# GpSimd's request queue held in program order in an expert layer that streams both of its tables

## The chip, the cores and the metric

The kernel runs on one core of one Trainium2 chip. The metric is the device time of one launch in microseconds. Five engines work side by side, each with its own instruction queue: TensorE (PE, with its weight loads shown as PEld), VectorE (DVE), ScalarE (ACT), GpSimd (POOL) and SyncE (SP). SP issues the plain loads from device memory, POOL issues the indirect ones, which fetch one table row per partition. The two share the core's 16 DMA engines.

## The reference

The program is one step of a two-layer encoder over 384 tokens: 256 of a prompt and 128 of eight sample streams. Layer 0 has a state-space mixer, layer 1 windowed attention; each is followed by a PEER channel mixer, and that is all that matters here:

```
s1, s2 = q1 @ sub_k1.T, q2 @ sub_k2.T          # 8 heads, 128 keys each
top 16 of s1, top 16 of s2, top 16 of the sums  # 128 experts of 16384 for each token
act = gelu(sum_d u_tab[eid] * x)                # one dot product per token and expert
out = sum_k (gate * act)[k] * v_tab[eid[k]]     # weighted sum of value rows
```

Both tables have 16384 rows of 1024 floats, 64 MB each, for each layer.

## The kernel before

**Two ways through the tables.** For the 256 prompt tokens the kernel computes all 16384 dot products densely, as matmuls of 128 blocks of the u table (`u_products`, lines 168 to 170), masks them with the gates (`w_prep`, `w_apply`, `w_mult`) and multiplies the result with 128 blocks of the v table (`v_products`, line 183). For the 128 sample tokens it fetches the chosen rows: each is one indirect DMA of 128 rows of 4 KB, 512 KB in all, issued by POOL at line 1250 (`gather`).

**Three kinds of request on POOL's queue.** `fetch_u` fetches a u row set, which DVE multiplies with the tokens in `u_item` (line 1299); 128 of them a layer, in a ring of 3 buffers (`gath`), and of 4 in the second part (`gathx`). `fetch_v` fetches a value row set into a freed place of the big arrays G0 and G1; four of them make a quad, which PE multiplies with small selection matrices `cm` in `v_quad` (line 1370); 24 quads, so 96 sets a layer. `fetch_item` fetches a value row set which DVE adds up itself in `v_item` (lines 1323 and 1325); 32 a layer. `items_end` (line 1339) adds DVE's sum to the quads' sum on PE. POOL also issues four plain DMAs a group of tokens (`load_group`, line 1071), one for the reload of the residual `h` (line 1618), and computes a few reciprocal roots.

**The steps.** Time within a layer is counted in steps s of one table block. Steps 0 to 63 are the first half of u, 64 to 127 the second half, 128 to 255 the values. In each step of the second half the program goes: gates of the step before, load and split of the blocks to come (`split`, lines 132 on ACT and 133 on DVE), products, `quads(s)`, `quads_ahead(s)` (which prepares `cm`), `w_prep`, `tick(s)`, and in the values `item_tick(s)`. A split is done two steps ahead of its products.

**What sets the requests.** `U_DUE` says how many u items are done by which step; `tick` fetches a set 2 or 3 items ahead of the item and runs it whatever the budget. `quads` issues one value set a step, if the budget `room` isn't negative and a place in `V_SLOTS` is free long enough (`v_slot`); a place is free again two steps after its quad. `V_DUE` holds the step of each quad: `quads_ahead` prepares it in the step before, `v_quad` runs in it. `PACE` refills the budget in each step, and each request takes 1 from it.

**What sets the order.** A planner arranges each engine's instructions by its own estimate of when they can start, unless they are held. From step 64 to the end of a layer the context `in_order` holds PE, DVE and ACT in program order (`HELD`, line 38). POOL and SP are not held: the planner may put a POOL request ahead of others that the program has before it, as long as its place is free. `load_group(1)` stands just ahead of step 64, outside the held stretch.

Of the kernel before, what the change touches and what calls it, by code (L numbers as in the profile page):

```python
# [26 lines left out]
HELD = (mybir.EngineType.PE, mybir.EngineType.DVE, mybir.EngineType.Activation)  # L27
# [16 lines left out]
TG = P // GR  # L44
# [12 lines left out]
GD = 2  # L57
QR = [r for r in range(32) if r // RG != GD]
I_DUE = (206, 250)
PACE = 1.6  # L60
AHEAD = 2 * 64 - 5
U_DUE = ((64, 22), (128, 68), (192, 115), (206, P))
V_DUE = [82, 85, 90, 95, 102, 148, 156, 162, 167, 171, 177, 181, 186, 192, 197, 203,
         213, 218, 223, 228, 233, 237, 243, 247]
V_SLOTS = [(1, e, 66, 64 + e) for e in range(28, 60, 4)] + [(0, e, 128 + e + 5, 256) for e in (0, 4, 8, 12, 20, 24, 28, 32, 56, 60)] + [(0, 16, 209, 256)]


# [1 line left out]
def encoder_step(ctx: ExitStack, tc: tile.TileContext, t_in, t_out):  # L69
# [14 lines left out]
    pin = tc.keep_in_program_order  # L84

    @contextmanager
    def in_order():

        traced = nc.cur_bb.bb.instructions
        n, last = len(traced), {}  # L90
        for i in traced:
            last[i.engine] = i
        kind = mybir.DependencyInfo(mybir.DependencyClass.NoSync, mybir.DependencyReason.DATA)
        yield
        for i in traced[n:]:
            if i.engine in HELD:
                if i.engine in last:
                    tc.add_manual_dep(i, last[i.engine].name, kind, reason="in order")
                last[i.engine] = i
# [844 lines left out]
    def peer(l):  # L944
        with ExitStack() as c:
# [56 lines left out]
            with in_order():  # L1002
                wq = [split_raw(raws[0])]
                sums(0, 0)
                sums(0, 1)
                sums(1, 0)
                nrm.rstd(0)
                nrm.scale(0, xn[0])
                sums(1, 1)
                sums(2, 0)  # L1010
                nrm.rstd(1)
                sums(2, 1)
                nrm.scale(1, xn[1])
                nrm.rstd(2)
                nrm.scale(2, xn[2], 2)
                for b in range(2):
                    turn(range(6), [b])
# [252 lines left out]
            def v_slot(n, s):  # L1270
                return next((k for *k, s0, s1 in V_SLOTS if s0 <= s and V_DUE[n // 4] <= s1 and taken.get(tuple(k), 0) <= s), None)

# [37 lines left out]
            def fetch_item(e2):  # L1310
                while spare[0] < 56 and spare[0] + 4 <= e2:
                    slots.append(spare[0])
                    spare[0] += 4
                if slots and done["g"] < TG and done["g"] < done["i"] + 3 and room[0] >= 0:
                    room[0] -= 1
                    j, e = done["g"], slots.pop(0)
                    items[j] = e, gather(G[0][:, e:e + 4].rearrange("p e t -> p (e t)"), t_in["p_v"], eidU[:, GD, j:j + 1])
                    done["g"] += 1

            def v_item(j):  # L1320
                e, row = items.pop(j)
                if j == 0:
                    pin(dve.tensor_scalar(acc, row, cU[:, 0:1], None, op0=OP.mult))
                else:
                    pin(dve.scalar_tensor_tensor(acc, row, cU[:, j:j + 1], acc, op0=OP.mult, op1=OP.add))
                slots.append(e)

            def items_sel():
                sel = T(one, [P, 4, 32], F32, tag="cm", bufs=2)
                dve.memset(sel, 0.0)  # L1330
                dve.tensor_reduce(sel[:, :, GD * RG:GD * RG + RG], ident.rearrange("p (q c r) -> p c r q", c=4, r=RG),
                                  axis=AX.X, op=OP.add)
                sels.append(sel)

            def items_end():
                sel = sels.pop()
                for hf in range(2):
                    for q in (3, 2, 1, 0):
                        pin(pe.matmul(out_s[hf][32 * q:32 * q + 32, :], sel[:, q], acc[:, hf * 512:hf * 512 + 512],
                                      start=False, stop=True, tile_position=(0, 32 * q)))  # L1340

            def item_tick(s):
                want = min(TG, max(0, TG * (s + 1 - I_DUE[0]) // (I_DUE[1] - I_DUE[0])))
                while done["i"] < want:
                    v_item(done["i"])
                    done["i"] += 1
                    if done["i"] == TG - 2:
                        items_sel()
                    if done["i"] == TG:
                        items_end()  # L1350
                if s >= I_DUE[0] - 4:
                    fetch_item(s - 2 * HE)

            def quad_prep(r):
                g = r // RG
                cm = T(one, [P, 4, 32], F32, tag="cm", bufs=2)
                dve.scalar_tensor_tensor(cm, ioh[:, None, 0:32].to_broadcast([P, 4, 32]), float(r),
                                         coef[g][:, r % RG::RG].unsqueeze(2).to_broadcast([P, 4, 32]),
                                         op0=OP.is_equal, op1=OP.mult)
                return r, cm  # L1360
# [12 lines left out]
            def u_weights(e2):  # L1373

                if e2 in NATIVE:
                    return load_raw(t_in["u_t"][l, e2]), None
                return load_split(t_in["u_t"][l, e2])
# [93 lines left out]
            done = {"u": 0, "v": 0, "f": 0, "i": 0, "g": 0, "c": 0}  # L1471
            cms, sels = [], []
# [4 lines left out]
            def tick(s):  # L1477

                room[0] = min(room[0] + PACE, PACE)
                s0, n0 = start[0], 0  # L1480
# [20 lines left out]
            def quads(s):  # L1501

                while cms:
                    v_quad(*cms.pop(0), s)
                    done["v"] += 1
                first = 4 * sum(d < 2 * HE for d in V_DUE)
                if (done["f"] < (first if s < 2 * HE else 4 * len(QR)) and room[0] >= 0 and v_slot(done["f"], s)):
# [3 lines left out]
            def quads_ahead(s):  # L1511

                while done["c"] < len(QR) and V_DUE[done["c"]] <= s + 1:
                    cms.append(quad_prep(QR[done["c"]]))
# [44 lines left out]

            turn_of.pop("v", None)  # L1560
            wt = u_weights(HE)
            held = in_order()
            held.__enter__()
            for e2 in range(HE):
                if mult:
# [27 lines left out]
            for e2 in range(2 * HE):  # L1593
# [17 lines left out]
                if e2 in w_at:  # L1611
                    made.append(w_prep(1, w_at[e2]))
                tick(2 * HE + e2)
                item_tick(2 * HE + e2)
                if e2 == AHEAD - 1:
                    lent.__exit__(None, None, None)
# [35 lines left out]

    mamba(t_in["x"].rearrange("(b p) d -> p b d", p=P))
    peer(0)
    attention()
    peer(1)
    final()

# [95 lines left out]
```

## Time and profile before

| | |
|---|---|
| median of 3 runs | 2385.33 us (2384.52 to 2387.32) |
| the profiled execution | 2389.37 us, span 2387.5 us |
| PE busy | 2317.2 us, 97% |
| DVE, ACT, POOL busy | 82%, 52%, 32% |
| mean DMA rate | 272 GB/s |
| second half of u and values, layer 0 | about 664 to 1306 us |
| the same, layer 1 | about 1732 to 2377 us |

A busy PE covers nearly the whole span, so what can be won without taking work from PE is the time in which it stands still or runs at a lower clock. The granted clock (PEclk) is a share of the full 2.4 GHz; 0.5 is the lower level of 1.2 GHz, and values between are means over a stretch that has both. The DMA share is the mean busy share of the 16 DMA engines, and it can show slightly over 1.

### The profile page before, as it was taken

The page shows a single profiled execution, that of the slowest core. Times are in us where ns is not written, and L with a number is a line of the kernel's source. Part 1 is how long each engine was busy: PE and PEld are TensorE (multiplying, and loading weights), DVE is VectorE, ACT ScalarE, POOL GpSimd, SP SyncE. Part 2 cuts the span into 40 slices and gives each one's busy share as a digit, 9 for nine tenths or more (in the row PEclk, how much of TensorE's full clock was granted, in tenths as well). Part 3 has the DMA queues.
Part 4 walks back from the last instruction along what each step waited for, and adds up shares of the span by engine and source line. Part 5 has one row for each costly group of instructions (what it writes and reads, how often), then busy time and mean ns, then how long its engine had stood idle before and what let it go on. Part 6 is the DMA issues. An engine that isn't in the chain of part 4 may idle for free.

```text
span 2387.5 us, 44460 instructions
## 1 busy us (share of the span) xinstructions
PE 2317.2 (97%) x16607; PEld 1984.0 (83%) x16607; DVE 1964.6 (82%) x4227; ACT 1252.3 (52%) x2428; POOL 772.6 (32%) x779
## 2 busy tenths in 40 slices
PE   7999999999989999999999999999989999999998
PEld 7899988999988997667777778999988997667676
DVE  5888855979978999888777676979978999887776
ACT  5656534344466766554444555344466766554343
POOL 2122200011144334556462200012144334566461
PEclk9999999999999999999999999999999999999999
DMA  5454435367689889999996515366789889999996
GB/s 200 174 193 172 150 142 170 117 205 254 237 311 343 302 300 336 382 399 405 377 414 253 166 65 180 124 218 241 249 316 343 295 306 333 395 395 413 343 417 250
DMA packets 177943, 649.75 MB, mean 272 GB/s; under 512 B 21232, under 2 KB 23136, under 8 KB 175328
## 3 DMA queue, kind: packets, MB, share of 16 engines
q1 hardware_dynamic: 100800, 365.85, 42.1%
q0 software_dynamic: 76928, 281.07, 31.4%
q8 instruction: 130, 2.13, 0.4%
q14 instruction: 85, 0.70, 0.1%
HBM read 630.62 MB, written 18.06 MB: 272 GB/s over the span
## 4 chain that ended last, share of the span: by engine, by line
PE 82%; DVE 6%; DMA 4%; issue 3%; ACT 2%; POOL 2%; another core or an unknown queue 0%; SPq 0%; POOLq 0%; DVEq 0%; ACTq 0%
PE bank L183 27%; PE bank L168 12%; PE bank L170 12%; PE bank L169 11%; PE bank L1370 3%; PE bank L1458 3%; PE bank L1383 2%; PE bank L1425 2%; DVE lo L133 2%; DMA gath<-in_p_u,eidU 1%; POOL G L1250 1%; DMA gathx<-in_p_u,eidU 1%; ACT hi L132 1%; DMA ab<-acum_rows 1%; PE bank L522 1%
## 5 line engine op out<-in xcount | busy, mean ns | idle before, releaser
L132 ACT CAST hi<-raw 128x1024 fp32r<-128x1024 f32 (+1 forms) x475 | 496.0, 1045 | 687.6 <-PE bank L169 322.7
L133 DVE TENSOR_TENSOR lo<-raw,hi 128x1024 fp32r<-128x1024 f32 (+1 forms) x475 | 576.0, 1213 | 171.8 <-ACT hi L132 159.0
L1250 POOL DMA_INDIRECT gath<-in_p_u,eidU x226 | 292.8, 1296 | 787.6 <-DVE gath L1299 455.3
L170 PE MATMUL bank<-xhi,lo 128*128 128x256 f32 (+1 forms) x1344 | 396.5, 295 | 17.0 <-DVE lo L133 15.8
L168 PE MATMUL bank<-xhi,hi 128*128 128x256 f32 (+1 forms) x1344 | 403.7, 301 | 0.4 <-issue 0.4
L169 PE MATMUL bank<-xlo,hi 128*128 128x256 f32 (+1 forms) x1344 | 394.8, 294 | 0.1
L1250 POOL DMA_INDIRECT G<-in_p_v,eidT x192 | 232.6, 1212 | 138.6 <-PE bank L1370 80.6
L170 PEld LDWEIGHTS bank<-xhi,lo 128*128 128x128 f32 x1344 | 255.7, 190 | 21.2 <-DVE lo L133 18.9
L168 PEld LDWEIGHTS bank<-xhi,hi 128*128 128x128 f32 x1344 | 256.0, 190 | 13.4 <-issue 7.9
L169 PEld LDWEIGHTS bank<-xlo,hi 128*128 128x128 f32 x1344 | 255.8, 190 | 1.5 <-issue 0.8
L168 PE MATMUL bank<-qhi,hi 128*128 128x256 f32 (+1 forms) x784 | 232.3, 296 | 0.0
L170 PE MATMUL bank<-qhi,lo 128*128 128x256 f32 (+1 forms) x784 | 227.0, 290 | 2.4 <-DVE lo L133 2.4
L169 PE MATMUL bank<-qlo,hi 128*128 128x256 f32 (+1 forms) x784 | 228.1, 291 | 0.0
L1413 ACT ACTIVATE oa<-ioh,e2T 128x128 f16<-128x128 f16 x512 | 163.6, 392 | 90.7 <-PE bank L1425 77.4
L132 ACT CAST hix<-raw 128x1024 fp32r<-128x1024 f32 x118 | 124.0, 1051 | 165.4 <-PE bank L183 76.9
L183 PE MATMUL bank<-hi,phi 128*128 128x512 f32 x632 | 204.6, 403 | 1.5 <-ACT phi L132 1.5
L183 PE MATMUL bank<-lo,phi 128*128 128x512 f32 x632 | 197.6, 392 | 0.9 <-DVE lo L133 0.9
L183 PE MATMUL bank<-hi,plo 128*128 128x512 f32 x632 | 196.3, 390 | 0.0
L133 DVE TENSOR_TENSOR lox<-raw,hix 128x1024 fp32r<-128x1024 f32 x118 | 144.1, 1221 | 16.8 <-ACT hix L132 16.5
L1299 DVE SCALAR_TENSOR_TENSOR gath<-gath,xg 128x1024 f32<-128x1024 f32 x114 | 138.7, 1217 | 16.5 <-DMA gath<-in_p_u,eidU 16.5
L183 PEld LDWEIGHTS bank<-hi,phi 128*128 128x128 f32 x632 | 113.9, 188 | 45.6 <-ACT phi L132 14.1
L170 PEld LDWEIGHTS bank<-qhi,lo 128*128 128x128 f32 x784 | 147.8, 188 | 2.8 <-DVE lo L133 2.8
(395 smaller groups left out, 5186.5 us busy)
## 6 DMA issues: line engine op xcount, KB each, us to landing
raw<-in_u_t SPq DMA_DIRECT2D x256, 512.0 KB
raw<-in_p_v SPq DMA_DIRECT2D x256, 512.0 KB
raw<-in_w_in SPq DMA_DIRECT2D x32, 512.0 KB
raw<-in_p_w_q SPq DMA_DIRECT2D x32, 512.0 KB
raw<-in_w_z SPq DMA_DIRECT2D x16, 512.0 KB
s<-in_state_ssm SPq DMA_DIRECT2D x8, 1024.0 KB
out_sm_ssm<-s SPq DMA_DIRECT2D x8, 1024.0 KB
raw<-in_w_out SPq DMA_DIRECT2D x16, 512.0 KB
```

The source lines that it names most:

```text
L132: act.copy(hi, raw)
L133: dve.tensor_tensor(lo, raw, hi32, op=OP.subtract)
L168: pe.matmul(ps, whi[:, s], xhi[:, k, c0:c1], start=(k == 0), stop=False)
L169: pe.matmul(ps, whi[:, s], xlo[:, k, c0:c1], start=False, stop=False)
L170: pe.matmul(ps, wlo[:, s], xhi[:, k, c0:c1], start=False, stop=(k == KD - 1))
L183: mm = pe.matmul(halves[hf], x, w[:, hf * n:(hf + 1) * n], start=s_, stop=e_)
L1250: pool.indirect_dma_start(out=tile_, out_offset=None, in_=tab, in_offset=bass.IndirectOffsetOnAxis(ap=idx, axis=0))
L1299: pin(dve.scalar_tensor_tensor(tile_, tile_, 1.0, xg[g], op0=OP.mult, op1=OP.mult, accum_out=au[g][:, j:j + 1]))
L1370: pe.matmul(out_s[hf][32 * q:32 * q + 32, :], cm[:, q], rows[q][:, hf * 512:hf * 512 + 512], start=(r == 0), stop=False, tile_position=(0, ...
L1383: pe.matmul(ps, wt[0][:, k * P:(k + 1) * P], xf[:, k], start=(k == 0), stop=(k == KD - 1))
L1413: act.activation(a[:, i], ioh, AF.Square, scale=-1.0, bias=e2T[:, t, 0:1])
L1458: pe.matmul(accs[b][hf], G[e2 // HE][:, e2 % HE, b * P:(b + 1) * P], wt[0][:, hf * 512:hf * 512 + 512], start=False, stop=False)
```

## The change

Three things are changed, and no instruction is added or taken away.

1. `in_order` takes the engines to hold as an argument, and the stretch from step 64 to the end of each layer now holds POOL as well. The dependencies that it adds are for the planner alone; they are no waits on the chip.
2. `PACE` goes from 1.6 to 1.5, and the steps of the value quads (`V_DUE`) are laid out anew: the first three stay, most of the others come 0 to 8 steps later, and the last is at 252 where it was at 247.
3. `items_end` now comes only when the last quad is done as well, which moves it from step 249 to step 252.

```
-PACE = 1.6
+PACE = 1.5
-V_DUE = [82, 85, 90, 95, 102, 148, 156, 162, 167, 171, 177, 181, 186, 192, 197, 203,
-         213, 218, 223, 228, 233, 237, 243, 247]
+V_DUE = [82, 85, 90, 96, 103, 148, 156, 162, 167, 173, 178, 183, 188, 193, 199, 211,
+         217, 222, 227, 232, 237, 243, 247, 252]
...
-    def in_order():
+    def in_order(engines=HELD):
...
         for i in traced[n:]:
-            if i.engine in HELD:
+            if i.engine in engines:
                 if i.engine in last:
                     tc.add_manual_dep(i, last[i.engine].name, kind, reason="in order")
                 last[i.engine] = i
...
-                    if done["i"] == TG:
-                        items_end()
+                if sels and done["i"] == TG and done["v"] == len(QR):
+                    items_end()
...
-            held = in_order()
+            held = in_order(HELD + (mybir.EngineType.Pool,))
```

## Rows read from the trace of the kernel before

**Rows 1.** The page's first part: busy time, share of the span and instructions of each engine.

```profile
PE 2317.2 (97%) x16607; PEld 1984.0 (83%) x16607; DVE 1964.6 (82%) x4227; ACT 1252.3 (52%) x2428; POOL 772.6 (32%) x779
```

**Rows 2.** Busy time by stretch, second half of u and values: stretch, its length, busy us of each engine (instructions), granted clock, DMA share, GB/s. Layer 0 first, then layer 1 from 1734.

```profile
666.00:702.00 36.00, 29.00 (x261) 27.80 (x260) 25.29 (x39) 19.52 (x41) 18.59 (x17) 0.91 0.91 343
756.00:762.00 6.00, 4.93 (x46) 4.52 (x44) 4.75 (x8) 4.52 (x10) 0.57 (x1) 1.00 1.03 414
895.00:1136.00 241.00, 241.00 (x1451) 167.82 (x1450) 213.50 (x360) 136.15 (x273) 132.68 (x109) 1.00 0.98 381
1136.00:1145.00 9.00, 6.56 (x37) 4.00 (x36) 4.72 (x8) 2.71 (x4) 3.75 (x4) 1.00 1.03 418
1145.00:1300.00 155.00, 155.00 (x749) 115.69 (x748) 119.41 (x150) 65.27 (x97) 74.43 (x57) 1.00 0.95 367
...
1734.00:1771.00 37.00, 29.60 (x268) 28.53 (x266) 25.96 (x39) 19.62 (x42) 18.68 (x17) 0.91 0.90 337
1826.00:1832.00 6.00, 5.17 (x55) 4.93 (x54) 5.92 (x11) 4.82 (x12) 0.29 (x1) 1.00 1.02 419
2205.00:2220.00 15.00, 10.88 (x49) 6.48 (x48) 9.40 (x16) 3.91 (x6) 5.15 (x4) 0.89 0.89 338
```

**Rows 3.** Who waited for whom: engine and line, what it waited for, us in total, times, longest. PE in the two layers' first part, then PE in their last part, then DVE at the start of layer 0's stretch.

```profile
PE bank L170 <- DVE lo L133: 7.7, 5, 5.7
...
PE bank L170 <- DVE lo L133: 7.2, 3, 5.9
...
PE bank L1370 <- DVE cm L1357: 2.4, 1, 2.4
...
PE bank L1370 <- DVE cm L1357: 4.1, 1, 4.1
...
DVE gath L1299 <- DMA gath<-in_p_u,eidU: 5.6, 1, 5.6
```

**Rows 4.** POOL's instructions in order of time at the start of layer 0's stretch: start, us, line, what, idle time before. Six more value requests stand between the second row and the third.

```profile
666.66 2.03 POOL L1071 DMA_DIRECT2D G<-xrow  x4 [2.02 <-ACT xlo L1534]
669.00 1.99 POOL L1250 DMA_INDIRECT G<-in_p_v,eidT  x1 [0.30 <-issue]
...
680.00 0.94 POOL L1250 DMA_INDIRECT G<-in_p_v,eidT  x1 [0.30 <-issue]
681.24 1.85 POOL L1250 DMA_INDIRECT gath<-in_p_u,eidU  x1 [0.30 <-issue]
```

**Rows 5.** Pieces of the chain that ended last, in order of time: start, us, what. For a DMA the time runs from its issue to its landing.

```profile
669.00 6.63 DMA G<-in_p_v,eidT
681.24 10.85 DMA gath<-in_p_u,eidU
...
951.07 1.85 PE bank L1370 x16
...
1105.53 1.95 PE bank L1370 x16
...
1129.21 9.92 DMA gathx<-in_p_u,eidU
...
1188.16 1.85 PE bank L1370 x16
...
1749.46 11.16 DMA gath<-in_p_u,eidU
...
2196.98 12.26 DMA gathx<-in_p_u,eidU
2212.23 3.45 PE bank L1370 x16
```

**Rows 6.** Busy time by stretch as in Rows 2, in pieces of 6 us after the halts at the two starts.

```profile
696.00:702.00 6.00, 6.00 (x36) 6.00 (x36) 4.22 (x7) 1.33 (x2) 0.84 (x1) 0.64 0.86 335
702.00:708.00 6.00, 6.00 (x66) 5.96 (x65) 5.57 (x10) 4.47 (x9) 1.03 (x2) 1.00 0.77 227
...
1764.00:1770.00 6.00, 6.00 (x35) 6.00 (x34) 4.22 (x8) 1.33 (x2) 0.94 (x1) 0.60 0.94 343
```

**Rows 7.** Instructions in order of time at the start of layer 0's stretch: DVE's u item of step 65, and ACT's cast of a u block at 680, with the idle time before it.

```profile
671.57 1.22 DVE L1299 SCALAR_TENSOR_TENSOR gath<-gath,xg 128x1024 f32<-128x1024 f32 x1
...
679.98 1.05 ACT L132 CAST hi<-raw 128x1024 fp32r<-128x1024 f32 x1 [3.30 <-remote]
```

**Rows 8.** POOL's instructions in order of time before the late halt in layer 1.

```profile
2191.78 0.94 POOL L1250 DMA_INDIRECT G<-in_p_v,eidT  x1 [1.56 <-PE bank L1370]
...
2195.52 1.16 POOL L1250 DMA_INDIRECT G<-in_p_v,eidT  x1 [0.30 <-DMA gath<-in_p_u,eidU]
2196.98 1.98 POOL L1250 DMA_INDIRECT gathx<-in_p_u,eidU  x1 [0.30 <-issue]
```

**Rows 9.** Groups of POOL's requests over the whole span: line, what, count, busy us and mean ns of one, idle time before and its causes.

```profile
L1250 POOL DMA_INDIRECT gath<-in_p_u,eidU x226 | 292.8, 1296 | 787.6 <-DVE gath L1299 455.3
L1250 POOL DMA_INDIRECT G<-in_p_v,eidT x192 | 232.6, 1212 | 138.6 <-PE bank L1370 80.6
```

**Rows 10.** The end of layer 1: two pieces of the chain, then DVE's first sums of the residual (line 1468) from the order of time.

```profile
2359.07 1.85 PE bank L1339 x16
2360.92 11.16 PE bank L183 x48
...
2374.66 1.28 DVE L1468 TENSOR_TENSOR h<-h,bank 128x512 f32<-128x512 f32 x2
```

## The prediction

> **What bounds the kernel now.** I read the busy shares first: PE is busy for 2317 of 2387.5 us [rows 1], and the change takes no work from it. So the question is where PE stands still inside the two stretches that the change touches, and the view by stretch says it: in layer 0, 36.0 - 29.0 = 7.0 us in the first 36 us, 1.07 us at 756, 2.44 us at 1136, and nothing in the two long pieces beside it; in layer 1, 37.0 - 29.6 = 7.4, 0.83 and 4.12 us [rows 2]. That is 22.9 us. The clock adds to it: after each starting halt PE runs for a few us at a lower granted clock, 0.64 and 0.60 in the mean of 6 us, and gets 36 and 35 products done where the next 6 us have 66 [rows 6]. That is 30/66 and 31/66 of 6 us, 2.7 and 2.8 us. In the late halt of layer 1 one quad took 3.45 us where others take 1.95 [rows 5], 1.5 us more. All that can be won without less work on PE is 22.9 + 5.5 + 1.5 = 29.9 us.
>
> Next, who holds PE there. At both starts it waits 5.7 and 5.9 us for line 133, DVE's low half of a u block [rows 3], though the block itself isn't late: DVE works in order, and just before it waits 5.6 us for a u row set [rows 3]. That set was issued at 681.24, because POOL had first issued `load_group` at 666.66 and then eight value requests from 669.00 to 680.00 [rows 4]. By the code those eight belong to steps 66 to 74, and their quads to steps 82 and 85: the planner took them first since their places were free. The u set then took 10.85 us to land, in layer 1 11.16 [rows 5]. The two late halts have the same form. A u set went out at 1129.21 and at 2196.98 and landed 9.92 and 12.26 us later [rows 5]; in layer 1 four value requests stand before it, from 2191.78 on [rows 8], which by the code belong to steps 202 to 210 (for the quad of step 213); DVE waits, its `cm` is late, and PE waits 2.4 and 4.1 us for that [rows 3].
>
> **The change, part by part.**
>
> *POOL in program order.* I followed `tick`, `quads`, `v_slot` and `fetch_item` by hand through steps 64 to 255 with the new constants. Behind `load_group(1)` comes the u set of step 65, then one value set, the u set of step 66, and so on in turn; the eighth value request comes in step 75. One request occupies POOL for 1.2 to 1.3 us [rows 9] and 0.3 us of issue [rows 4]. The u set that was issued at 681.24 now has three requests in front of it (`load_group`, one u set, one value set) and a buffer that comes free when DVE has done the item of step 65, begun at 671.57 [rows 7]. So it goes out in about 673, some 8 us earlier, and the halt for it, 5.6 us on DVE, is covered. I take the whole of 5.7 + 5.9 on PE and the clock with it, 5.5: 17.1 us. What is late next are the u blocks: ACT waited 3.30 us for one at 680 [rows 7], and that accounts for the other 1.3 + 1.5 us of the two starts. In that time the DMA engines had nine requests and the blocks; now it is seven and the blocks. I take half of the 2.8, 1.4 us. Bounds: nothing (the blocks wait as before), or all.
>
> The Trainium skill, "DMA: Bandwidth & Descriptors", section "Queues, rings and completion order", says that each DMA engine takes turns between the queues that have work, a packet at a time. By that rule SP's blocks had their share of turns however many value requests POOL had queued, so fewer of these would not bring them sooner: the 1.4 us would be zero, and the sum 1.4 us smaller. The rule leaves the u set's own delay as it is, since that stood behind the eight in the same queue.
>
> *The halts at 756 and 1826* (1.07 and 0.83 us) come in a stretch at DMA share 1.03 [rows 2] after two batches of four value requests. In program order these are one a step. Half of it, 1.0 us; bounds 0 and 1.9.
>
> *The late halts.* The u sets of steps 192 to 206 come at 13 in 14 steps. The value requests beside them become fewer: the quad of step 203 goes to 211 and the next from 213 to 217, so steps 200 to 207 have 9 requests of all kinds where the code had 10, and none from later steps are put in front. Four requests fewer are 4 x 0.524 MB / 420 GB/s = 5 us of DMA time (the most that rows 2 show is 419), against waits of 2.4 and 4.1. The total is 2.4 + 4.1 + 1.5 = 8.0 us; I take two thirds, 5.4, because the ring of four buffers still has to turn 0.93 sets a step. Bounds 0 and 8.0.
>
> *The new waits.* Held in order, a request whose buffer isn't free keeps all behind it back. Queued behind it are the other kinds of gather; who waits for those are DVE (u and item rows) and PE (quads). A u set waits for the item 3 or 4 before it, so POOL can be ahead of the program by one to two steps at most. Counted so, the 96 value sets have at least 4.9 steps from the latest release that stands before them to the end of their quad's step; 12 of them have 4.9 or 5.0, the others more. A step is (1105.53 - 951.07) / 44 = 3.5 us from step 148 to 192, and (1188.16 - 1105.53) / 26 = 3.2 with its halt, 3.1 without, from 192 to 218 [rows 5]. So the least is 4.9 x 3.1 = 15.2 us, less two requests that POOL issues before it, 3 us: 12.2 us. The landings on the chain took 6.6 to 12.3 us [rows 5], the longest with the DMA engines full and more requests ahead than the new order has. PE's quads should be covered, with no margin at the longest row. I charge 2 us for both layers; bounds: 0, and the rival below.
>
> The Trainium skill, same page, section "Anatomy of one DMA — SWDGE (gpsimd) path", gives about 2.0 us plus the bytes at 436 GB/s, an estimate of 3.2 us for one such request alone. No row here shows one alone; by that figure the rows above are mostly queue, an even pace would shorten them, and the 2 us would be 0.
>
> *The pace and the later quads.* The number of requests, quads and instructions is as before, so PE's and POOL's work is too. `items_end` and the last quad come 3 and 5 steps later. Before, `items_end` was over at 2360.92, and 11.16 us of products (four steps) followed before the last pair; the first sums of the residual ran at 2374.66 [rows 10]. Three of these four steps now come first, so the sum is ready about 2.8 us before 2372, some 5 us before DVE asks for it. Cost nothing; without that cover, one quad and one `items_end`, 3.8 us. The reload of `h` follows the last value request in the queue, and that one's place is free since the end of step 247, before the buffers that `h` replaces: nothing.
>
> **Sum.** 17.1 + 1.4 + 1.0 + 5.4 - 2.0 = 22.9 us. The profiled execution took 2389.37 us (span 2387.5), 4.0 more than the median of 2385.33; its halts are no different in kind, so I take the sum off both: 2366.5 for a profiled run, and **2362.4** for the median, call it 2362.
>
> **The rivals.**
>
> *The starting halt only changes its cause.* The blocks of u are what is late at 680 [rows 7], `load_group(1)` still stands ahead of all, and PE waits for a block instead of for DVE. Half of the start's 17.1 + 1.4 is won and little elsewhere: some 9 us, 2376. Against it: in the long wait DVE stood on the row set, while ACT's wait was over at 680.
>
> *The quads' rows are late.* This is the one that ends slower. Before, the rows for the quads of the values were issued in batches, as soon as PE gave the places back, far ahead: those issued from 2191.78 are for the quad of step 213, and the quad of step 203 ran at 2212.23 [rows 5, 8], so ten steps of 3.1 us later, in about 2243, their own turn came, 51 us after the issue. Now the last of a quad have 12 us. If landings in the full stretches (0.98 DMA share, [rows 2]) take more than 12.2 us, PE itself waits at line 1370, at each of the 19 quads of a layer's values. At 1 us each that is 38 us, against 18.5 won at the starts: 2385 + 19.5 = 2405. It decides from a landing of 12.2 us; for it speaks the row of 12.26, against it that this row had hoisted requests in front.
>
> *No change to speak of.* The new dependencies would not bind the indirect DMAs, or the waits return one for one in other places, for the DMA engines are at 0.94 to 1.03 in these stretches anyway [rows 2]. Only the layout of the quads would count, a few us either way: 2384.
>
> **How the numbers follow.** Forecast 0.62; the halt that changes its cause 0.13; late quads 0.15; no change 0.10. 0.2% of the median, 4.8 us, is about what a measurement of this kernel can tell from no change. Faster: 0.62 and most of the second case, 0.12, is 0.74; the same: 0.01 + 0.10 = 0.11; slower 0.15. The low end of the range is all that can be won, 2385.3 - 29.9 = 2355, with 2 us for the other order's effect on the planner elsewhere: 2353. The high end takes in the second case and no change, 2385 with 1 us for the spread of the runs, 2386; outside it is little but the case of the late quads.
>
> **What would show it.** Right: in POOL's order of time u and value requests in turn from about 669; the u set that was at 681 out before 675; no wait of PE on line 133 over 2 us and no low clock after either start; PE idle in the two stretches down from 22.9 us to under 8. Wrong: PE's quads (line 1370) waiting on a DMA or on POOL; DVE waiting more than before for row sets; ACT waiting longer than 3.3 us for a block at the start. The prediction falls if the median is above 2381, or if PE's idle time goes and the time does not.

## The result, and the profile after

The changed kernel takes 2359.9 us (median of 5 runs, 2357.42 to 2365.42), the kernel before 2385.33 (5 runs, 2384.52 to 2387.32). The ratio is 0.9888, 95% interval 0.9874 to 0.9902: faster by 1.1%, 25.4 us. The prediction was 2362. The profiled execution of the changed kernel took 2358.57 us with a span of 2356.7; the spans differ by 30.8 us.

The page's first part, answering to [rows 1]: PE is busy 11 us less, with the same instructions (one record is missing).

```profile
PE 2306.2 (98%) x16606; PEld 1979.3 (84%) x16607; DVE 1964.8 (83%) x4227; ACT 1251.5 (53%) x2428; POOL 764.1 (32%) x779
```

Busy time by stretch, columns as in [rows 2]: the start of layer 0's second half of u, the place of the first quads, the late stretch of the values, then the same three places in layer 1.

```profile
665.40:701.40 36.00, 35.50 (x372) 34.73 (x371) 34.05 (x52) 27.18 (x58) 23.14 (x20) 1.00 0.97 373
743.00:749.00 6.00, 6.00 (x67) 5.96 (x66) 5.45 (x9) 4.47 (x9) 2.76 (x3) 1.00 0.98 345
1110.00:1122.00 12.00, 12.00 (x61) 8.54 (x60) 9.86 (x16) 4.42 (x8) 7.50 (x7) 1.00 1.02 410
...
1719.70:1757.00 37.30, 34.73 (x365) 33.95 (x363) 33.24 (x50) 26.49 (x57) 20.62 (x20) 1.00 0.98 371
1800.00:1806.00 6.00, 6.00 (x66) 5.96 (x66) 5.45 (x10) 4.44 (x10) 1.97 (x2) 1.00 0.94 330
2165.00:2180.00 15.00, 15.00 (x74) 11.01 (x73) 12.83 (x21) 6.79 (x10) 9.07 (x9) 1.00 1.02 413
```

Two columns matter. PE is busy 35.50 of 36.00 us where it was busy 29.00, and the granted clock of that stretch is 1.00 where it was 0.91. And PE's instruction count rises from 261 to 372 in the same 36 us: 42% more instructions, though the busy time rose by 22% only. The count also shows what the busy time hid at 756: 46 matmuls before [rows 2], 67 now.

POOL's instructions in order of time at the start of layer 0's stretch, columns as in [rows 4].

```profile
666.07 2.03 POOL L1071 DMA_DIRECT2D G<-xrow  x4 [4.47 <-ACT xlo L1534]
668.40 1.99 POOL L1250 DMA_INDIRECT gath<-in_p_u,eidU  x1 [0.30 <-issue]
670.69 1.14 POOL L1250 DMA_INDIRECT G<-in_p_v,eidT  x1 [0.30 <-issue]
672.40 0.94 POOL L1250 DMA_INDIRECT gath<-in_p_u,eidU  x1 [0.57 <-DVE gath L1299]
673.65 1.05 POOL L1250 DMA_INDIRECT G<-in_p_v,eidT  x1 [0.30 <-issue]
675.00 0.94 POOL L1250 DMA_INDIRECT G<-in_p_v,eidT  x1 [0.30 <-issue]
676.25 1.33 POOL L1250 DMA_INDIRECT gath<-in_p_u,eidU  x1 [0.30 <-issue]
```

From 668.40 on one or two value sets stand between two u sets, and the u set that went out at 681.24 [rows 4] goes out at 672.40, 8.8 us earlier. The one before it, which the planner had put ahead of `load_group(1)` (at 662.79), now follows it, 5.6 us later; in layer 0 DVE waits 0.9 us for row sets there, in layer 1 still 2.5. What is left of the waits of [rows 3], in the same form (PE in layer 0's first part and in layer 1's, DVE at the start of layer 0 and of layer 1):

```profile
PE bank L170 <- DVE lo L133: 1.4, 3, 0.5
...
PE bank L170 <- DVE lo L133: 3.3, 4, 2.1
...
DVE gath L1299 <- DMA gath<-in_p_u,eidU: 0.9, 2, 0.5
...
DVE gath L1299 <- DMA gath<-in_p_u,eidU: 2.5, 1, 2.5
```

In the last parts PE waits neither for `cm` nor for a DMA. The late wait of DVE for a row set is gone as well: in layer 0 from 1080 to 1180 it had 5.1 us for `gathx` and 4.4 for `gath` before, and has none now.

**Where the time went.** A single execution of this kernel also drifts in places that the change doesn't touch, so I compare stretches between fixed instructions. A runs from the start of `load_group(1)` (POOL, line 1071) to the first quad (PE, line 1370, step 82); B from there to the third quad (step 90); C from there to the first reciprocal root behind the values (POOL, line 211); M from that root in layer 0 to `load_group(1)` of layer 1, which no held stretch covers. Here are the marks of the kernel before in layer 0 after 666.66 [rows 4], from its order of time, and then the changed kernel's after 666.07, layer 0 and layer 1:

```profile
734.64 1.92 PE L1370 MATMUL bank<-G,cm 128*32 128x512 f32 x16
...
765.15 1.92 PE L1370 MATMUL bank<-G,cm 128*32 128x512 f32 x16
...
1305.24 0.56 POOL L211 TENSOR_TENSOR rstd<-ss,mhalf 128x1 f32<-128x1 f32 x1 [17.03 <-DVE ss L210]
```

```profile
724.59 1.92 PE L1370 MATMUL bank<-G,cm 128*32 128x512 f32 x16
...
752.71 1.92 PE L1370 MATMUL bank<-G,cm 128*32 128x512 f32 x16
...
1289.81 0.56 POOL L211 TENSOR_TENSOR rstd<-ss,mhalf 128x1 f32<-128x1 f32 x1 [18.71 <-DVE ss L210]
...
1720.59 2.03 POOL L1071 DMA_DIRECT2D G<-xrow  x4 [4.47 <-ACT xlo L1534]
...
1780.57 1.92 PE L1370 MATMUL bank<-G,cm 128*32 128x512 f32 x16
...
1808.69 1.92 PE L1370 MATMUL bank<-G,cm 128*32 128x512 f32 x16
...
2346.42 0.56 POOL L211 TENSOR_TENSOR rstd<-ss,mhalf 128x1 f32<-128x1 f32 x1 [18.71 <-DVE ss L210]
```

So A of layer 0 is 724.59 - 666.07 = 58.52 us. In the table, each row is one profiled execution, in us, layer 0 / layer 1; the ratio is to the kernel before on the same chip. The experiments are described below.

| kernel | A | B | C | M | ratio (95%) |
|---|---|---|---|---|---|
| before | 67.98 / 68.14 | 30.51 / 30.55 | 540.09 / 543.43 | 429.64 | 1 |
| changed | 58.52 / 59.98 | 28.12 / 28.12 | 537.10 / 537.73 | 430.78 | 0.9888 (0.9874 to 0.9902) |
| e1 order only | 57.55 / 59.13 | 28.12 / 28.13 | 538.40 / 538.58 | 433.24 | 0.9891 (0.9876 to 0.9906) |
| e2 layout only | 66.10 / 68.53 | 28.13 / 28.12 | 539.34 / 540.67 | 431.38 | 0.9978 (0.9969 to 0.9987) |
| e3 order in u only | 57.70 / 58.44 | 28.13 / 28.12 | 542.49 / 542.90 | 436.57 | 0.9914 (0.9898 to 0.9930) |
| e4 burst at the start | 68.87 / 68.64 | 28.13 / 28.13 | 537.11 / 537.11 | 431.19 | 0.9958 (0.9944 to 0.9971) |
| e5 order in values only | 66.99 / 68.88 | 28.12 / 28.13 | 537.14 / 537.30 | 430.31 | 0.9949 (0.9934 to 0.9963) |
| e6 quads 1 step earlier | 58.45 / 58.82 | 28.12 / 28.12 | 539.28 / 537.70 | 429.37 | 0.9897 (0.9878 to 0.9916) |
| e7 quads 2 steps earlier | 58.02 / 59.01 | 28.13 / 28.13 | 542.17 / 542.81 | 436.72 | 0.9918 (0.9903 to 0.9933) |
| e8 no pace | 60.21 / 59.56 | 28.12 / 28.12 | 539.11 / 541.60 | 431.39 | 0.9925 (0.9907 to 0.9942) |
| e10 four at once, late | 58.13 / 61.32 | 28.13 / 28.13 | 537.66 / 537.30 | 433.50 | 0.9891 (0.9875 to 0.9906) |
| e11 four at once, always | 58.70 / 59.23 | 28.13 / 28.26 | 546.98 / 546.25 | 431.22 | 0.9973 (0.9961 to 0.9985) |

e9 moves the first mark of A and is compared where it is told of. How far single executions scatter can be read from the rows: C is 537.1 to 537.7 us in the changed kernel, e4 and e5, which treat the values alike, while A is 57.6 to 60.2 us in layer 0 and 58.4 to 61.3 in layer 1 wherever POOL is held at the start and no burst is put there. The 30.8 us between the two spans are then: A -9.46 and -8.16, together -17.6; B -2.39 and -2.43, -4.8; C -2.99 and -5.70, -8.7; M +1.1; before 666 and behind the last root -0.8. Of the 30.8, 4.0 are no gain of the change, since the profiled run of before lay that much above its median, and 1.3 because the changed kernel's lay below its own: 25.4 by medians.

### The profile page after: what moved, and what is told of

Its sections match the earlier page's. It is cut to its first block, busy times and chain, and to the rows that moved or that the text cites. A ratio compares the mean times of both kernels' runs of the same rounds, so it can differ in the third digit from the quotient of the medians.

```text
span 2356.7 us, 44413 instructions
## 1 busy us (share of the span) xinstructions
PE 2306.2 (98%) x16606; PEld 1979.3 (84%) x16607; DVE 1964.8 (83%) x4227; ACT 1251.5 (53%) x2428; POOL 764.1 (32%) x779
## 5 line engine op out<-in xcount | busy, mean ns | idle before, releaser
L1250 POOL DMA_INDIRECT G<-in_p_v,eidT x192 | 223.8, 1166 | 78.5 <-issue 53.3
L169 PEld LDWEIGHTS bank<-qlo,hi 128*128 128x128 f32 x784 | 148.9, 190 | 0.4
```

Of the source, the lines that this page charges most:

```text
L169: pe.matmul(ps, whi[:, s], xlo[:, k, c0:c1], start=False, stop=False)
L1250: pool.indirect_dma_start(out=tile_, out_offset=None, in_=tab, in_offset=bass.IndirectOffsetOnAxis(ap=idx, axis=0))
```

## The experiments

**Taking the change apart (e1, e2).** e1 is the kernel before with POOL held in order and nothing else; e2 is the changed kernel with POOL left to the planner.

```diff
 e1, against the kernel before:
-            held = in_order()
+            held = in_order(HELD + (mybir.EngineType.Pool,))
 e2, against the changed kernel:
-            held = in_order(HELD + (mybir.EngineType.Pool,))
+            held = in_order()
```

> Before with POOL held in program order from step 64 on, and nothing else: pace 1.6, the old steps of the quads, items_end at step 249. Theory (the order is what wins; pace and layout matter little): 2357 to 2364 us, PE idle at both starts and at the late halts gone as in the changed kernel. Rival (the order removes the starting halts, pace and layout the late ones): the starts gone, the late halts of 2.4 and 4.1 us with their clock still there, 2366 to 2370. Rival (pace is what wins): 2380 to 2386.

> The changed kernel with POOL left to the planner: pace 1.5, the new steps of the quads and items_end at 252 stay. Theory (order): the planner again puts eight value requests ahead of the u set at both starts, PE waits 5 to 6 us there and then has the low clock; 2376 to 2386. Rival (layout removes the late halts): the starts stay and the late halts go, 2374 to 2378. Rival (pace alone evens the requests): 2360 to 2366.

The order alone gives 0.9891, the whole change 0.9888: with the order in place, the new pace and layout bring nothing that these intervals tell apart (C is 0.9 to 1.3 us better with them, A 0.9 to 1.0 worse, which is within A's scatter). The layout alone gives 0.9978, some 5 us. POOL's order of time in e2 shows why its starts are as slow as before's: the planner again takes eight value requests ahead of the u set.

```profile
665.32 2.03 POOL L1071 DMA_DIRECT2D G<-xrow  x4 [2.02 <-ACT xlo L1534]
667.64 2.00 POOL L1250 DMA_INDIRECT G<-in_p_v,eidT  x1 [0.30 <-issue]
...
678.54 1.97 POOL L1250 DMA_INDIRECT G<-in_p_v,eidT  x1 [0.30 <-issue]
680.81 1.43 POOL L1250 DMA_INDIRECT gath<-in_p_u,eidU  x1 [0.30 <-issue]
```

PE's largest waits in e2, at the starts of layer 0 and layer 1 and late in each layer, have the old form; only the late ones are smaller than in [rows 3].

```profile
PE bank L170 <- DVE lo L133: 7.4, 3, 6.7
...
PE bank L170 <- DVE lo L133: 8.9, 2, 8.5
...
PE bank L1370 <- DVE cm L1357: 0.6, 1, 0.6
...
PE bank L1370 <- DVE cm L1357: 1.0, 1, 1.0
```

Stretch B is 28.12 us in both, so either half of the change removes the halts at 756 and 1826. What made them is not shown. It was not the two batches of four value requests by themselves: e2 still issues both (733.60 to 738.29 and 744.89 to 748.98) and has no halt, and in the kernel before DVE waits for no row set from 735 to 765. The waits there, by the trace's semaphores, are of DVE and ACT for PE, and of PE for line 133, 0.9 us.

**Where the order counts (e3, e5).** e3 holds POOL in steps 64 to 127 only, e5 in the values only. Both keep the new pace and layout.

```diff
 e3, at the end of the second half of u (e5: the two ways of holding exchanged):
             u_gelu(*gelu.pop())
+            held.__exit__(None, None, None)
+            held = in_order()
+            held.__enter__()
```

> The changed kernel with POOL held in program order in steps 64 to 127 only; the values are left to the planner again, pace and layout stay as changed. Theory: starts and the halts at 756 and 1826 stay away; late halts come back in part, since value requests go out early again in the steps 192 to 206, against a layout that has fewer of them there: 2360 to 2367. If the late halts hang on the layout alone: 2358 to 2362, PE idle as in the changed kernel.

> The changed kernel with POOL held in program order in the values only (step 128 on); the second half of u is left to the planner. Theory (each stretch has its own share): both starting halts are back, 66 to 69 us from load_group(1) to the first quad where the changed kernel has 58.5 and 60.0, and the values run as in the changed kernel, 351.3 us from the quad of step 148 to the first root after them; 2374 to 2380. Rival (the halts of the values come from a backlog that the second half of u leaves behind): the values are slower too, 353 us and more, 2378 to 2386.

The starts follow the order in u: A is 57.7 and 58.4 us in e3, 67.0 and 68.9 in e5. C follows the order in the values: 537.1 and 537.3 us in e5. Each half wins by itself, and in A and C each does what the whole does.

e3 was a miss: its median is 2369.82 us where 2360 to 2367 was expected, and its late part went further than freedom in the values explains: C is 542.5 and 542.9, longer than e2's 539.3 and 540.7, with the same layout and the same freedom there. PE's waits in e3's late parts, layer 0, then layer 1:

```profile
PE bank L183 <- DVE lo L133: 3.6, 3, 2.8
...
PE bank L183 <- DVE lo L133: 3.7, 2, 3.2
...
PE bank L1370 <- DVE cm L1357: 0.9, 1, 0.9
```

In these parts DVE waits for row sets (up to 6.7 us in one piece). The planner's order in the values depends on what stands before it; why it came out worse here than in e2 is left open.

**The start by itself (e4).** Held in order throughout, but the program itself now issues eight value sets in step 66, as the planner had done.

```diff
-                if (done["f"] < ... and room[0] >= 0 and v_slot(done["f"], s)):
-                    fetch_v(done["f"], s)
-                    done["f"] += 1
+                for i in range(8 if s == HE + 2 else 1):
+                    if (done["f"] < ... and (i or room[0] >= 0) and v_slot(done["f"], s)):
+                        fetch_v(done["f"], s)
+                        done["f"] += 1
```

> The changed kernel, held in order, but with the first eight value requests all in step 66, ahead of that step's u set, as the planner had them. Theory (the burst ahead of the u set makes the starting halt): the halt is back in both layers, DVE waits about 5 us for the row set, PE 5 to 6 us for line 133, then the low clock; 2374 to 2380. Rival (the burst is harmless, the gain comes from the order later on or from the blocks of u coming sooner): 2358 to 2364.

A goes back to 68.9 and 68.6 us, B and C stay as in the changed kernel. The gain of the starts is thus the place of the u set in POOL's queue: it is issued at 683.21, behind the burst. The waits tell the rest: DVE's at layer 0's start, then PE's at the two layers' starts.

```profile
DVE gath L1299 <- DMA gath<-in_p_u,eidU: 9.3, 1, 9.3
...
PE bank L170 <- DVE lo L133: 9.4, 3, 8.8
...
PE bank L170 <- DVE lo L133: 9.3, 2, 8.9
```

Busy time by stretch in e4, columns as in [rows 2]:

```profile
696.00:702.00 6.00, 6.00 (x38) 6.00 (x37) 4.22 (x8) 1.33 (x2) 0.94 (x1) 0.66 0.93 348
702.00:708.00 6.00, 6.00 (x66) 5.96 (x65) 5.97 (x11) 4.46 (x9) 0.94 (x1) 1.00 0.67 216
```

After the 8.8 us halt the granted clock is 0.66 for a piece of 6 us and 38 products are done where the next piece has 66, as in [rows 6]. But ACT waits for no block of u here: its waits from 660 to 705 are for PE alone.

Nor was a block late in the kernel before. The 3.30 us of [rows 7] carry no name: "remote" says that the profile knows no releaser. The trace's semaphores settle it. The cast at 679.98 waited for three: the one that the block's load raises was last raised at 670.56, DVE's at 678.56 and PE's at 679.99. In layer 1 the cast at 1748.29 has the load at 1739.59 and PE at 1748.30. So both blocks had landed some 9 us before, and ACT waited for PE.

**How far the new waits are (e6, e7).** The quads of the values come one step earlier (e6), then two (e7), with the requests as they are.

```diff
-V_DUE = [82, 85, 90, 96, 103, 148, 156, ..., 247, 252]
+V_DUE = [82, 85, 90, 96, 103, 147, 155, ..., 246, 251]      e7: 146, 154, ..., 245, 250
```

> The changed kernel with the quads of the values one step earlier against their requests (steps 147, 155, 161 ...). In the changed kernel the last row set of a quad was issued 11.7 to 19.1 us before its use; here the least is about 8.6 us. Theory of the prediction (landings of 10 to 12 us when the DMA engines are full, decision near 12.2): PE waits at line 1370 for the rows of several quads, 0.5 to 3 us each, and the values take 355 us or more; 2362 to 2385. Rival (paced requests land within 8 us, the long landings of before were its own queue): no wait at line 1370, 2357 to 2364.

> The same with the quads two steps earlier, the least about 5.5 to 6 us before use. Theory of the prediction: PE waits 3 to 6 us at most quads, the values take over 375 us a layer, 2400 and more. Rival (paced requests land within 8 us): some waits of up to 2 us, 2360 to 2385; if they land within 5 us, none.

In the changed kernel the least time from a value set's issue to its quad, its lead, is 11.8 us. Its two instructions, from the order of time:

```profile
1203.66 0.94 POOL L1250 DMA_INDIRECT G<-in_p_v,eidT  x1 [0.31 <-issue]
...
1215.42 1.92 PE L1370 MATMUL bank<-G,cm 128*32 128x512 f32 x16
```

No quad waits there. One step earlier costs 2.2 us of C in layer 0 and nothing in layer 1. PE waits for row sets there, 0.5 us in layer 1 and 2.1 in layer 0 (for 1.3 of these the profile names an item of DVE, but that quad's last row set landed 0.13 us before the quad began). Two steps earlier cost 5.1 us in each layer, and the median of 2369.03 us is far below the 2400 that the prediction's theory gave. PE's waits in e7's late parts, layer 0 and layer 1 (the edit makes the line numbers one less):

```profile
PE bank L1369 <- DMA G<-in_p_v,eidT: 4.8, 4, 1.8
...
PE bank L1369 <- DMA G<-in_p_v,eidT: 4.6, 5, 2.7
```

And one of these quads, in the order of time of e7:

```profile
1201.02 1.86 POOL L1249 DMA_INDIRECT G<-in_p_v,eidT  x1 [0.30 <-issue]
...
1212.25 1.07 PE L1369 MATMUL bank<-G,cm 128*32 128x512 f32 x8 [1.64 <-DMA G<-in_p_v,eidT]
```

The quad stands still until its row set is there, so the landing is read from it: 1212.25 - 1201.02 = 11.2 us. Over all quads that waited in e6 and e7 it was 7.6 to 11.2 us. With two steps less PE waits 4 times in layer 0 and 6 in layer 1 (one of these, 0.2 us, before the late part), of 19 quads of the values in each.

For a part of the requests the traces also hold the landing itself. The line of a kind of request gives their number and the median us from issue to landing; here are u sets and value sets of the changed kernel, then the value sets of e2, whose POOL is left to the planner.

```profile
gath<-in_p_u,eidU POOLq DMA_INDIRECT x226, 6.7
G<-in_p_v,eidT POOLq DMA_INDIRECT x192, 8.5
...
G<-in_p_v,eidT POOLq DMA_INDIRECT x192, 7.4
```

In the changed kernel 73 of the 192 value sets can be read: their landings took 5.2 to 13.05 us, eight of them more than 11.7. The tightest took 12.60 us with a lead of 13.61 and so came 1.0 us before its quad. The margin is thus not that every landing stays under the least lead, but that the slow ones met longer leads. And the order did not make landings quicker: the median is 7.4 and 7.6 us where the planner is free in the values (e2, e3) and 8.3 to 9.2 in all others that can be read. Why isn't shown.

**The pace (e8).** The budget is taken away, so that a request goes out as soon as there is a place for it.

```diff
-PACE = 1.5
+PACE = 8
```

> The changed kernel, held in order, with a pace of 8 requests a step, so that the budget never binds: a value set goes out in every step in which a place is free. Theory (the order wins, the pace does little): 2357 to 2365, values 351 to 354 us. Rival (the pace keeps the u sets of steps 192 to 206 ahead of the value sets): late halts of 2 to 4 us are back in each layer, 2364 to 2372.

The ratio is 0.9925 and C is 2.0 and 3.9 us longer. By the code, the value sets then go out as places come free, in order but not evenly among the u sets and items, and PE waits once a layer, at line 1281, for a matrix that DVE prepares late (line 1306, in a buffer of `cm`), 1.2 us in layer 0 and 1.4 in layer 1. Where the rest went isn't shown. So the pace is worth something once the order is kept, though 1.5 against 1.6 is not.

**Still less at the start (e9).** `load_group(1)` goes from the front of the stretch to the u item of step 68.

```diff
-            load_group(1)
...
-                if k == TG + 8:
-                    load_group(2)
+                if k in (TG - 8, TG + 8):
+                    load_group(k // TG + 1)
```

> The changed kernel with load_group(1) issued with the u item of step 68 (its rows are first used in step 76) instead of ahead of step 64, so that the u set of step 65 no longer stands behind it. Theory (what PE still loses at the start, 58.5 and 60.0 us from load_group(1) to the first quad, is the rest of that queue): 1 to 2 us less in the second layer, nothing in the first: 2356 to 2362, a difference that the timing alone can't show, so the stretch up to the first quad decides, counted from the last cast of the first half. Rival (the four plain DMAs at the start delay nothing): the same stretch.

This was a miss. Counted from ACT's cast that stands before `load_group(1)` in the changed kernel (line 1534), the first quad comes after 63.1 and 64.2 us, in the changed kernel after 59.4 and 60.9: about 3.5 us later in each layer (the other kernels with a held start and no burst have 58.5 to 61.1 and 59.3 to 62.2), with DVE waiting 3.6 and 4.8 us for u sets. The group now stands among the requests of a full stretch (677.18) instead of ahead of them; that this is the reason is likely, but no run tests it. The ratio, 0.9898 (0.9883 to 0.9914), shows no gain.

**Batches late in the layer (e10, e11).** e10 issues four value sets at once in step 198 and charges the budget for each. e11 issues up to four in every step of the values in which places are free; those behind the first go out whatever the budget is and are not charged, so that the budget no longer paces the value sets.

```diff
 e10; e11 has  4 if s >= 2 * HE else 1  and gives the charge back,  room[0] += i > 0:
+                for i in range(4 if s == 198 else 1):
+                    if (done["f"] < ... and (i or room[0] >= 0) and v_slot(done["f"], s)):
```

> The changed kernel, held in order, with the four value sets of the quad of step 211 all issued in step 198, ahead of that step's u set, where the changed kernel has them in steps 198, 200, 202 and 208. Theory (value requests ahead of u sets make the late halts): DVE waits for u row sets between steps 198 and 206, PE loses 1 to 4 us there in each layer, values 352.5 to 355 us where the changed kernel has 351.3. Rival (the late halts came from the DMA engines being full for long, four requests more make none): 351 to 352 us. Start and first half as in the changed kernel; 2359 to 2368 in all.

> The changed kernel, held in order, but in the values the sets of a quad go out four at a time as soon as their places are free, as the planner had them before (batches in steps 150, 158, 164, 169, 175, 180, 185, 190, 195, 201, 213 and so on); only the first of a batch takes from the budget. The single late batch of the run before made DVE wait 3.5 us for a row set and cost PE 0.2 to 0.4 us. Theory (late halts come from batch upon batch ahead of the u sets): DVE waits several times between steps 190 and 206, PE loses 1 to 6 us there, values 353 to 358 us where the changed kernel has 351.3, 2362 to 2374 in all. Rival (batches in order are harmless, it was the planner's order of u sets and items among themselves): 351 to 352 us.

One batch makes DVE wait 3.5 us for the u set behind it (3.4 in layer 1), but PE loses nothing that stretch C shows: 537.7 and 537.3 us. I had expected 1 to 4 us. A split is done two steps ahead of its products, which can cover such a wait. Batch on batch does not go unseen: C is 547.0 and 546.3 us, 9.9 and 8.5 more than the changed kernel's, worse than before the change and more than I had expected; the median of 2382.34 us lies above the 2362 to 2374 that were forecast. DVE's late wait for u sets in layer 0 of e11 (three in all), then PE's late waits, layer 0 and layer 1:

```profile
DVE gath L1299 <- DMA gath<-in_p_u,eidU: 16.3, 3, 6.7
...
PE bank L183 <- DVE lox L133: 6.0, 2, 3.6
...
PE bank L183 <- DVE lox L133: 7.0, 2, 5.7
```

and one of its stretches, columns as in [rows 2]:

```profile
1110.00:1160.00 50.00, 44.04 (x197) 32.76 (x196) 35.22 (x54) 18.45 (x29) 23.88 (x18) 0.93 0.95 366
```

The changed kernel has PE busy for all of the same 50 us, with 239 matmuls and clock 1.00. The DMA share is 0.95 in e11, 1.02 there: the engines have no more to do, the u sets just come behind the batches. The rival theory, that the late halts came from too much DMA traffic in those steps and not from its order, predicts no such loss from the number of requests, which is the same over the layer. The missing pace alone doesn't make the loss either: e8, whose budget never binds but which issues one value set a step at most, loses 2.0 and 3.9 us.

No kernel of these beats the changed one clearly; the intervals of e1, e6, e9 and e10 overlap its own.

## Why the prediction was right, point by point

**The bound and the cause of the starts: right.** PE's idle time behind a late u set, and that set behind eight value requests in POOL's queue, were what could be won at the starts. e4 brings the burst back and with it the 10.3 and 8.7 us of A; e2 and e5, where the planner is free in u, are as slow. The sum said 17.1 + 1.4 = 18.5 us for both layers, A shows 17.6. Its parts fit too: over A in both layers PE's idle time falls by 11.0 us, where 11.6 were counted for the wait, and its busy time by 6.6 with the clock of A going from 0.95 to 1.00, where 5.5 were counted for the clock. The signs named in advance came out but for two small ones: the u set went out at 672.40 behind just the three requests that were named, and PE's idle time over A to C is 7.5 us, under 8; but at times two value sets stand between u sets, and in layer 1 PE still waits 2.1 us once for line 133, behind a row set that came 2.5 us late.

**The 1.4 us for blocks that come sooner: wrong as a step.** It was said that fewer requests would bring the u blocks sooner. But no block was late: the wait at 680 was read as one for a block, and by the semaphores it was for PE, 9.4 us after the block had landed. e4 has the burst and no wait for a block either. The measured 17.6 lies by the 17.1 without that term. The Trainium skill, "DMA: Bandwidth & Descriptors", section "Queues, rings and completion order", has it that each DMA engine takes turns between the queues that have work. The traces agree: eight requests on POOL's queue delayed the u set behind them and not SP's blocks.

**The halts at 756 and 1826: under-sized, 1.0 against 4.8 us, and their cause not shown.** The term was half of PE's idle time, 1.07 + 0.83. But the 6 us at 756 had 46 matmuls [rows 2] where an undisturbed piece has 66 [rows 6], and 20/66 of 6 us is 1.8 us, not 1.07. The ends of matmuls are modelled, so the idle column is only a lower bound of a halt. Over B, 2.4 us a layer were lost, half of it in busy time, and all of it was won. The prediction put them down to two batches of requests; e2 has the same batches and no halt.

**The late halts: right in cause, 5.4 against 8.7 us.** C shows more than the whole 8.0 of which two thirds were taken. e5, which holds POOL in the values alone, has the C of the changed kernel, and e11 brings long halts back with batches in front of u sets, though without the pace as well; the single batch of e10 costs nothing. What the prediction put down to fewer requests, four of them by the new layout, was mostly the order: e1, with the old layout, wins 1.7 and 4.9 us of C, e2, with the new layout and no order, 0.8 and 2.8.

**The new waits: charged at 2 us, measured none.** The 12.2 us of least lead that was counted from the code is 11.8 in the trace. That the longest landings belonged to the old order was wrong: four of the 73 that can be read in the changed kernel took more than 12.2 us. PE waited for none of them, as their leads were 13.6 to 35 us. This is also where the rival of the late quads fails. Landings beyond its point of decision did occur, but its step from "a landing can exceed 12.2 us" to "each of the 19 quads waits 1 us" leaves out that a quad waits only when its own set is late, and slow landings and short leads rarely met. e7 shows the price: 5.1 us a layer with every lead two steps shorter. That they didn't meet at all in the changed kernel, with 1.0 us between them at the tightest, is in part luck.

The Trainium skill's figure gives an estimate of 3.2 us for one such request ("Anatomy of one DMA — SWDGE (gpsimd) path" of the same page). It held for none of those that can be read in the changed kernel: the landings of 192 of its 512 requests, most of them issued in A to C at a DMA share of 0.94 to 0.96, took 4.2 to 13.05 us. An even pace did not shorten the queue, and the 2 us went to 0 for another reason: the leads just sufficed.

**The pace and the later quads: nothing, right beside the order.** e1 against the changed kernel shows no difference. Without the order the layout wins 0.22%, some 5 us, where the rival of no change to speak of gave it 1 us (2384).

**The sum.** 22.9 us were predicted; the medians show 25.4 and the two profiled spans 30.8. The terms do not all agree as well as the total: the starts fit to 1 us, B and C were under-sized by 3.8 and 3.3, the waits over-sized by 2. That adds up to a gain 8 us larger than predicted in the stretches A to C, 31.1 for 22.9. That the median came within 2.1 us of the 2362 is therefore luck in part: by medians the total came out nearer, since the profiled run of before lay 4.0 us above its median and the changed kernel's 1.3 below. Where in the trace of before these 4.0 us lie can't be told from one execution, so part of what B and C seem to have given may be theirs.

## What to carry to other kernels

On a queue that serves several consumers, what counts is what stands ahead of the urgent request. Here a planner that fills free places first put eight requests that could wait before the one that PE depended on, and that cost 8 to 9 us at each start; holding the queue in program order was enough, and without a pace in that order a part of the gain was lost. Before such a hold, count from the issue to the use of each request and compare it with landings under load, request by request. Don't take a wait without a named releaser for a late load: see which semaphore ended it. And size a halt by the number of instructions done in a stretch against an undisturbed one, not by its idle time.

## What was not expected of the hardware

The same stretch of nearly the same program differs by several us between executions. M, the attention and the first half of u, took 430.8 us in the changed kernel and 436.6 in e3, though both have the same instructions there in the same order on PE, DVE and ACT. All of M by stretch, columns as in [rows 2], the changed kernel and then e3:

```profile
1289.81:1720.59 430.78, 417.11 (x3198) 384.61 (x3198) 350.78 (x1166) 206.83 (x436) 55.47 (x75) 1.00 0.52 176
```

```profile
1294.52:1731.09 436.57, 423.24 (x3198) 389.62 (x3198) 351.17 (x1166) 207.23 (x436) 54.80 (x75) 0.98 0.50 174
```

PE's idle time is nearly the same in both, 13.7 and 13.3 us; the busy time is 6.1 us longer in e3, where the mean granted clock is 0.98 and not 1.00, so part of it is spent at the lower of the two levels. e7 has 0.98 there and M 436.7. What decides it isn't shown here. It is why single executions were compared stretch by stretch, and not by their totals: 6 us of M is more than most of the edits above are worth. Whether the other executions of e3 and e7, from which their ratios come, had the lower clock too is not in a trace.
